# A two-block transformer on one core: first loads reordered, small tables issued behind x, and the adaLN modulation split 7 + 5 between two layers

## The chip, the cores and the metric

One Trainium2 chip; the program runs on one of its cores. The metric is device time in microseconds (us) of one execution. All arithmetic is float32. A float32 product is done as three TensorE passes: each operand is split into a high part `hi` (rounded to the type that TensorE reads in one pass) and a rest `lo = x - hi`, and `hi*hi + hi*lo + lo*hi` is accumulated.

## The reference, cut to what matters

There are 256 tokens of width 1024. A first block has two layers; a second block with state-space and sparse-attention mixers follows. A vector `c` of length 1024 modulates the second block:

```python
def first_block(x, mem, ...):
    x = layer_norm(x, emb_ln_g, emb_ln_b)
    for l in range(2):
        mixed = hybrid_mixer(x, mem, ...)      # conv, differential attention, attention over mem
        x = layer_norm(ALPHA * x + mixed, ln1_g[l], ln1_b[l])
        ff = square(relu(x @ w_up[l])) @ w_down[l]          # 1024 -> 4096 -> 1024
        x = layer_norm(ALPHA * x + ff, ln2_g[l], ln2_b[l])

def second_block(x, c, ...):
    mod = silu(c) @ ada_w + ada_b              # 1024 -> 6144, needs nothing of the first block
    shift_m, scale_m, gate_m, shift_f, scale_f, gate_f = split(mod, 6)
    h = rmsnorm(x, pre_norm_mix) * (1.0 + scale_m) + shift_m
    ...
```

`memory_attention` in both layers needs `mem @ w_mem_kv[l]` (256 x 1024 by 1024 x 512), which depends on no token.

## The kernel before, in words

**Weights.** Every weight arrives in units of 128 x 2048 floats (1 MB). `weight(...)` (line 242) loads a unit over SyncE's DMA queue into one of two `raw` buffers, in `parts` pieces, and then, in chunks of `cut` columns (1024 by default), ScalarE copies `raw` to `hi` (L255) and VectorE subtracts to `lo` (L256). There are four pairs of `hi`/`lo` buffers. So a load waits for a `raw` buffer that VectorE has finished with, and a split waits for a `hi`/`lo` pair that TensorE has finished with. The products are recorded on L261, L262 and L263, the transposes of tokens on L340.

**Order.** The program states operations and tiles. A planner in the compiler simulates the machine by its own cost figures and writes a fixed order of instructions for each engine and each DMA queue; the program's order is the priority among what the plan holds ready. At run time each engine and queue follows its fixed order, so an instruction whose operand is late holds up all behind it on its engine.

**Start.** `load()` brings `mem` (four pieces of 256 KB), the value weights of `mem` for layer 0 (two pieces of 512 KB), its key weights (1 MB), `x` (two of 512 KB) and the two rows of the first layer norm (512 KB each, as every partition gets a copy), all on SyncE's queue. `columns()` and `toeplitz()` bring small tables on GpSimd's queue: `cols` (256 KB), two copies of packed rows (32 and 256 KB), `shp` (224 KB), `hot` (64 KB) and `rb` (0.5 KB). None depends on anything, so they are issued in the first microseconds. GpSimd also does the power -0.5 of each layer norm (L309).

**Feed-forward of a layer.** Eight steps of 512 hidden channels. In step j the loop computes `up(j+1)` (two weight units, 96 matmuls of 256 columns) and the two `down` units of step j (48 matmuls of 512 columns), so that TensorE always has the next step's activations. After the loop come `up(7)` and the last four `down` units (12 to 15), with `close(t)` (residual, layer norm, transposes into `xT`) for each half of the tokens. PSUM holds four accumulators all the while.

**Modulation.** `silu(c) @ ada_w` is done on VectorE, not TensorE, in 12 parts of 512 columns. `modulation_part(n)` (L762) loads four pieces of 512 KB over SyncE's queue (L773) into two buffers tagged `s`, multiplies by a scalar of each partition and adds up (L777 once, L779 seven times), transposes 32 x 32 blocks (L781) and reduces (L782) into 16 columns of `modr`:

```python
        for h in range(4):
            w = self.new("s", [128, 2, 512])
            nc.sync.dma_start(out=w, in_=a["ada"][n, h])
            for k in range(2):
                ...   # acc (+)= w[:, k, :] * silu_c
        vec.transpose(out=t, in_=acc)
        vec.tensor_reduce(out=self.modr[:, 16 * n:16 * n + 16], ...)
```

Parts 0 to 5 lie in the six loop steps of layer 0, parts 6 to 11 in those of layer 1. `modulation_end()` sums the partitions with four small products on TensorE (L792, from `modr` and a table `place`), adds the bias (L795, L798), transposes (L800) and writes the gates out. Its result `modc` is first read in `modulated(0, ...)`, right after the first `close` of layer 1.

The functions that the diff touches, and what calls them:

## Time and profile before

| | before |
|---|---|
| median of 3 runs | 1275.21 us (1273.62 to 1282.3) |
| the profiled execution's own time | 1279.33 us |
| its span in the trace | 1277.6 us |
| TensorE matmul busy | 1203.1 us (94%) |
| VectorE busy | 966.1 us (76%) |
| ScalarE busy | 662.8 us (52%) |
| mean granted TensorE clock | 0.982 |
| moved by DMA | 247.81 MB, 194 GB/s on average |

The trace is one execution on the core. Times in it count from the span's start. "Busy" of TensorE is modelled from pipelined matmuls, so it is no measure of how near the engine is to its peak; gaps are read from the starts of instructions.

### The profile page before, as it was taken

How to read it: one execution, taken by the hardware profiler on the slowest of the kernel's cores; microseconds unless marked ns; L12 is line 12 of the kernel's file. 1: busy time of each engine (PE TensorE's matmuls, PEld its weight loads, DVE VectorE, ACT ScalarE, POOL GpSimd, SP SyncE). 2: the span in 40 equal slices, each digit the busy share in tenths (PEclk: the TensorE clock that was granted, in tenths of full speed). 3: DMA queues.
4: the chain of work that ended last, by engine and by line, in shares of the span. 5: the costliest groups of instructions: out<-in, count | busy, mean ns of one | idle time of the engine just before them, and what ended most of it. 6: DMA issues, size and time to landing. Idle time of an engine off the chain costs nothing.

```text
span 1277.6 us, 20408 instructions
## 1 busy us (share of the span) xinstructions
PE 1203.1 (94%) x8031; PEld 1064.6 (83%) x8031; DVE 966.1 (76%) x1741; ACT 662.8 (52%) x1082; POOL 65.2 (5%) x75
## 2 busy tenths in 40 slices
PE   6997989999999899999988899999999999999997
PEld 5886679899888568998877788789999968899996
DVE  5898577777789667787768995389999987655553
ACT  4546754444353875444335577555555634544441
POOL 2100000000000000000001000000111110000000
PEclk9998999999999899999989999999999999999999
DMA  8733567777561556777735344165454534554450
GB/s 310 263 138 122 191 217 261 253 294 278 198 239 67 190 189 242 273 272 256 279 105 192 120 161 167 70 243 190 164 185 185 185 110 159 198 199 180 183 198 33
DMA packets 53425, 247.81 MB, mean 194 GB/s; under 512 B 5277, under 2 KB 17597, under 8 KB 30545
## 3 DMA queue, kind: packets, MB, share of 16 engines
q1 hardware_dynamic: 52256, 243.22, 53.0%
q0 software_dynamic: 1072, 3.28, 0.8%
q8 instruction: 63, 1.03, 0.3%
q14 instruction: 34, 0.27, 0.1%
HBM read 241.06 MB, written 6.47 MB: 194 GB/s over the span
## 4 chain that ended last, share of the span: by engine, by line
PE 59%; DVE 18%; DMA 11%; ACT 7%; issue 4%; POOL 0%; SPq 0%; DVEq 0%; ACTq 0%; POOLq 0%
PE mm L263 11%; PE mm L262 11%; PE mm L261 11%; PE acc L263 7%; PE acc L261 7%; PE acc L262 6%; DVE lo L256 6%; DMA raw<-in_wts 6%; DVE cy L512 3%; DMA s<-in_ada 3%; ACT hi L255 3%; PE tr L340 1%; DVE t L779 1%; DMA rel<-reld 1%; DVE mask L1015 1%
## 5 line engine op out<-in xcount | busy, mean ns | idle before, releaser
L255 ACT ACTIVATE hi<-raw 128x1024 fp32r<-128x1024 f32 (+1 forms) x367 | 367.3, 1025 | 376.0 <-DMA raw<-in_wts 169.8
L256 DVE TENSOR_TENSOR lo<-raw,hi 128x1024 fp32r<-128x1024 f32 (+1 forms) x367 | 431.6, 1185 | 153.5 <-ACT hi L255 152.9
L261 PE MATMUL mm<-xT,hi 128*128 128x256 f32 x992 | 282.8, 285 | 2.6 <-DVE zs L1147 1.5
L263 PE MATMUL mm<-xT,lo 128*128 128x256 f32 x992 | 282.5, 285 | 0.0
L262 PE MATMUL mm<-xT,hi 128*128 128x256 f32 x992 | 282.1, 284 | 0.0
L261 PEld LDWEIGHTS mm<-xT,hi 128*128 128x128 f32 x992 | 191.8, 193 | 5.1 <-DVE zs L1147 1.7
L262 PEld LDWEIGHTS mm<-xT,hi 128*128 128x128 f32 x992 | 191.7, 193 | 0.8
L263 PEld LDWEIGHTS mm<-xT,lo 128*128 128x128 f32 x992 | 191.9, 193 | 0.2
L261 PE MATMUL acc<-hi,mh 128*128 128x512 f32 x320 | 127.8, 399 | 5.3 <-ACT mh L599 5.3
L262 PE MATMUL acc<-lo,mh 128*128 128x512 f32 x320 | 126.4, 395 | 0.0
L263 PE MATMUL acc<-hi,mh 128*128 128x512 f32 x320 | 125.9, 394 | 0.0
L262 PE MATMUL mm<-lo,xT 128*128 128x256 f32 (+1 forms) x288 | 85.7, 298 | 2.1 <-DVE lo L256 2.1
L263 PE MATMUL mm<-hi,xT 128*128 128x256 f32 (+1 forms) x288 | 86.4, 300 | 1.2 <-DVE xT L346 1.2
L261 PE MATMUL mm<-hi,xT 128*128 128x256 f32 (+1 forms) x288 | 87.1, 302 | 0.1
L779 DVE SCALAR_TENSOR_TENSOR t<-s,silu_c,t 128x512 f32<-128x512 f32 x84 | 62.9, 749 | 30.8 <-DMA s<-in_ada 30.3
L263 PE MATMUL mm<-h,lo 128*128 128x256 f32 x288 | 80.6, 280 | 0.0
L261 PE MATMUL mm<-h,hi 128*128 128x256 f32 x288 | 80.3, 279 | 0.0
L262 PE MATMUL mm<-h,hi 128*128 128x256 f32 x288 | 80.3, 279 | 0.0
L261 PEld LDWEIGHTS acc<-hi,mh 128*128 128x128 f32 x320 | 60.9, 190 | 18.7 <-ACT mh L599 6.1
L263 PEld LDWEIGHTS acc<-hi,mh 128*128 128x128 f32 x320 | 60.5, 189 | 13.8 <-issue 1.4
L262 PEld LDWEIGHTS acc<-lo,mh 128*128 128x128 f32 x320 | 60.7, 190 | 12.5 <-issue 1.1
L261 PEld LDWEIGHTS mm<-hi,xT 128*128 128x128 f32 x288 | 55.5, 193 | 5.2 <-issue 1.8
(382 smaller groups left out, 2220.7 us busy)
## 6 DMA issues: line engine op xcount, KB each, us to landing
raw<-in_wts SPq DMA_DIRECT2D x174, 1024.0 KB
s<-in_ada SPq DMA_DIRECT2D x48, 512.0 KB
rel<-reld SPq DMA_DIRECT2D x64, 64.0 KB
bias<-bo SPq DMA_DIRECT2D x16, 256.0 KB
bias<-bias SPq DMA_DIRECT2D x8, 512.0 KB
cr<-cumd SPq DMA_DIRECT2D x8, 512.0 KB
mh<-in_wts SPq DMA_DIRECT2D x3, 1024.0 KB
row<-in_ln_g SPq DMA_DIRECT2D x4, 512.0 KB
```

The costliest lines, as they stand in the source:

```text
L255: nc.scalar.activation(h[:, s], raw[:, s], AF.Copy)
L256: (lo_on or nc.vector).tensor_tensor(out=l[:, s], in0=raw[:, s], in1=h[:, s].bitcast(F32), op=OP.subtract)
L261: t.matmul(out=out, lhsT=l[0], rhs=r[0], start=start, stop=False)
L262: t.matmul(out=out, lhsT=l[0], rhs=r[1], start=False, stop=False)
L263: t.matmul(out=out, lhsT=l[1], rhs=r[0], start=False, stop=stop)
L340: self.nc.tensor.transpose(out=p[:, i, :], in_=x[:, i * 128:i * 128 + 128], identity=self.ident)
L512: vec.scalar_tensor_tensor(out=y, in0=u[:, c, j:j + 256], scalar=tap(j), in1=y, op0=OP.mult, op1=OP.add)
L779: vec.scalar_tensor_tensor(out=acc, in0=w[:, k, :], scalar=s, in1=acc, op0=OP.mult, op1=OP.add)
L1015: vec.scalar_tensor_tensor(out=isc, in0=rl[:, i, :], scalar=self.widx[:, t, h:h + 1], op0=OP.mult, op1=OP.add, in1=self.nadm[:, t, :] if h ...
```

## The change

1. `load()`: the value weights of `mem` for layer 0 come first, in four pieces of 256 KB with splits of 512 columns; `mem` goes to ScalarE's DMA queue.
2. `run()`: a one-column copy on GpSimd that reads `x[0]` is put ahead of `columns()` and `toeplitz()`, and every GpSimd instruction of these two is ordered behind it (`issue_after` adds order on that engine, no semaphore).
3. `layer()`: layer 0 takes modulation parts 0 to 6 (part 6 behind `up(7)`), layer 1 parts 7 to 11 in its first five steps; `modulation_end()` moves behind `up(7)` of layer 1.

```diff
     def load(self):
-        ms = []
+        wv = self.weight("mem", 0, 1, parts=4, cut=512)
         for t in range(NT):
             m = self.new("s", [128, D])
             for h in range(2):
-                nc.sync.dma_start(out=m[...], in_=a["mem"][...])
+                nc.scalar.dma_start(out=m[...], in_=a["mem"][...])
                 self.split_t(m[:, 512 * h:512 * h + 512], self.memT, 4 * h, t)
-            if t == 0:
-                wv = self.weight("mem", 0, 1, parts=2)
         wk = self.weight("mem", 0, 0)
...
+        self.gate = self.b1.tile([128, 1], F32, name="gate")
...
     def layer(self, l):
             hs.append(up(j + 1))
-            self.modulation_part(6 * l + j)
-            if 6 * l + j == 11:
-                self.modulation_end()
+            if 7 * l + j < 12:
+                self.modulation_part(7 * l + j)
             for i in range(2):
                 w = self.weight("down", l, 2 * j + i)
...
         hs.append(up(7))
         g, b = self.row(a["ln2_g"], D * l), self.row(a["ln2_b"], D * l)
         last = l + 1 == DEPTH
+        if last:
+            self.modulation_end()
+        else:
+            self.modulation_part(6)
...
     def run(self, stop=None):
             self.load()
-            self.columns()
-            self.toeplitz()
+
+            gate = nc.gpsimd.tensor_copy(self.gate, self.x[0][:, 0:1])
+            with tc.issue_after(gate.ins):
+                self.columns()
+                self.toeplitz()
```

## Rows read from the trace of the kernel before

**Rows 1.** The page's head and its first part: busy time of an engine, share of the span, instructions.

```profile
span 1277.6 us, 20408 instructions
PE 1203.1 (94%) x8031; PEld 1064.6 (83%) x8031; DVE 966.1 (76%) x1741; ACT 662.8 (52%) x1082; POOL 65.2 (5%) x75
```

**Rows 2.** Who waited for whom between 510 and 645 us, the feed-forward of layer 1: total us, how often, the longest.

```profile
PE tr L792 <- DVE modr L782: 7.3, 1, 7.3
```

**Rows 3.** TensorE's instructions in order of time near the end of layer 1's feed-forward: start us, us, engine, line, operation; in brackets the idle time before and what ended it.

```profile
635.48 0.28 PE L262 MATMUL mm<-xT,hi 128*128 128x256 f32 x1
643.03 1.94 PE L792 MATMUL tr<-modr,t 128*128 128x48 f32 x8 [7.27 <-DVE modr L782]
...
650.88 0.40 PE L261 MATMUL acc<-hi,mh 128*128 128x512 f32 x1
```

**Rows 4.** Busy time by stretches of 3 us there: stretch, length, then busy us (instructions) of PE, PEld, DVE, ACT and POOL, the granted TensorE clock, DMA share, GB/s.

```profile
636.00:639.00 3.00, 0.00 (x0) 0.00 (x0) 1.05 (x2) 1.03 (x2) 0.00 (x0) 0.96 0.72 274
639.00:642.00 3.00, 0.00 (x0) 0.00 (x0) 3.00 (x4) 1.30 (x2) 0.00 (x0) 0.50 0.10 41
...
645.00:648.00 3.00, 3.00 (x15) 2.96 (x16) 2.33 (x8) 0.63 (x1) 0.00 (x0) 0.50 0.25 104
```

**Rows 5.** VectorE's instructions in order of time, the ends of parts 10 and 11 and the wait in part 11.

```profile
616.57 0.69 DVE L782 TENSOR_REDUCE modr<-t 128x16 f32<-128x512 f32 x1
...
637.95 0.75 DVE L779 SCALAR_TENSOR_TENSOR t<-s,silu_c,t 128x512 f32<-128x512 f32 x1 [3.93 <-DMA s<-in_ada]
...
642.29 0.69 DVE L782 TENSOR_REDUCE modr<-t 128x16 f32<-128x512 f32 x1
```

**Rows 6.** TensorE in order of time, three first matmuls of `down` units: of step 0 in layer 0, of units 12 to 15 (behind the six steps) in layer 0, and of step 5 in layer 1.

```profile
200.82 0.40 PE L261 MATMUL acc<-hi,mh 128*128 128x512 f32 x1
...
335.34 0.40 PE L261 MATMUL acc<-hi,mh 128*128 128x512 f32 x1
...
617.26 0.40 PE L261 MATMUL acc<-hi,mh 128*128 128x512 f32 x1
```

**Rows 7.** The instructions of the modulation parts on VectorE, over the span: duration in ns (min/median/max), first and last start. The third is a group of 331 to 337 us: count, busy us, mean ns.

```profile
L779 DVE SCALAR_TENSOR_TENSOR t<-s,silu_c,t x84: 744/749/755, 203.8 to 639.8; 128x512 f32<-128x512 f32 x84
...
L777 DVE TENSOR_SCALAR t<-s,silu_c x12: 480/481/483, 199.7 to 620.6; 128x512 f32<-128x512 f32 x12
...
L781 DVE STREAM_TRANSPOSE t<-t 128x512 f32<-128x512 f32 x1 | 0.7, 707 | 0.0
...
L782 DVE TENSOR_REDUCE modr<-t x12: 685/686/689, 218.4 to 642.3; 128x16 f32<-128x512 f32 x12
```

**Rows 8.** Busy time by stretches at the end of layer 0's feed-forward (columns as in rows 4).

```profile
331.00:337.00 6.00, 6.00 (x46) 5.71 (x45) 4.97 (x6) 3.25 (x5) 0.00 (x0) 1.00 0.54 184
337.00:345.00 8.00, 8.00 (x37) 6.64 (x36) 4.39 (x6) 3.00 (x4) 0.00 (x0) 1.00 0.71 262
345.00:351.00 6.00, 6.00 (x28) 4.74 (x27) 5.71 (x13) 1.79 (x2) 0.92 (x1) 1.00 0.00 0
351.00:357.00 6.00, 5.99 (x30) 4.89 (x30) 6.00 (x7) 3.43 (x5) 0.00 (x0) 1.00 0.16 59
```

**Rows 9.** The same place in order of time, one row or two of SyncE's queue, VectorE, ScalarE and TensorE each: the last piece of part 5 issued, and waited for; a `down` unit issued, and waited for; TensorE at the second half's layer norm.

```profile
322.76 0.33 SPq L773 DMA_DIRECT2D s<-in_ada  x1
...
325.69 0.33 SPq L249 DMA_DIRECT2D raw<-in_wts  x1
...
328.24 0.75 DVE L779 SCALAR_TENSOR_TENSOR t<-s,silu_c,t 128x512 f32<-128x512 f32 x1 [1.91 <-DMA s<-in_ada]
...
333.18 1.06 ACT L255 ACTIVATE hi<-raw 128x1024 fp32r<-128x1024 f32 x1 [4.16 <-DMA raw<-in_wts]
...
365.08 1.29 PE L340 MATMUL tr<-ident,x 128*128 128x128 f32 x8 [0.79 <-DVE x L362]
```

**Rows 10.** Busy time by stretches at the start (columns as in rows 4).

```profile
0.00:4.00 4.00, 0.38 (x2) 0.41 (x3) 0.00 (x0) 1.28 (x1) 3.04 (x11) 1.00 0.42 141
4.00:8.00 4.00, 1.75 (x8) 1.02 (x6) 0.00 (x0) 0.00 (x0) 2.48 (x7) 1.00 0.95 261
8.00:12.00 4.00, 0.00 (x0) 0.00 (x0) 1.25 (x2) 2.17 (x3) 0.00 (x0) 1.00 1.02 356
12.00:16.00 4.00, 2.94 (x12) 2.65 (x13) 3.21 (x6) 1.03 (x3) 0.00 (x0) 1.00 0.99 386
...
20.00:24.00 4.00, 3.89 (x32) 3.89 (x33) 4.00 (x8) 0.80 (x3) 0.00 (x0) 1.00 1.03 426
...
28.00:32.00 4.00, 3.58 (x28) 3.16 (x27) 4.00 (x9) 3.68 (x6) 0.00 (x0) 1.00 0.41 138
```

**Rows 11.** The start in order of time, rows of GpSimd, ScalarE, VectorE and TensorE: a table issued, the first weights split, the first product, the `lambda` table used, the key weights of `mem`, the statistics of `x`, the first power -0.5.

```profile
3.52 0.56 POOL L399 DMA_DIRECT2D shp<-in_shp  x1
...
9.16 1.06 ACT L255 ACTIVATE hi<-raw 128x1024 fp32r<-128x1024 f32 x1 [7.14 <-DMA raw<-in_wts]
...
12.48 0.58 PE L261 MATMUL mm<-hi,mh 128*128 128x256 f32 x1 [6.73 <-ACT mh L345]
...
14.32 0.42 DVE L404 TENSOR_TENSOR t<-t 128x256 f32<-128x256 f32 x1
...
14.77 0.48 DVE L406 TENSOR_REDUCE sm<-t 128x2 f32<-128x128 f32 x2
...
17.14 1.06 ACT L255 ACTIVATE hi<-raw 128x1024 fp32r<-128x1024 f32 x1 [4.11 <-DMA raw<-in_wts]
...
21.71 1.87 DVE L329 BATCH_NORM_STATS2 sm<-x 128x6 f32<-128x512 f32 x3
...
24.45 0.94 POOL L309 TENSOR_TENSOR sm<-sm,mhalf 128x1 f32<-128x1 f32 x1 [17.97 <-DVE sm L333]
```

More of the change, by code (lines that the diff above doesn't have):

```diff
@@ L440, in load @@
             for h in range(2):
-                nc.sync.dma_start(out=m[:, 512 * h:512 * h + 512], in_=a["mem"][0, t * 128:t * 128 + 128, 512 * h:512 * h + 512])
+                nc.scalar.dma_start(out=m[:, 512 * h:512 * h + 512], in_=a["mem"][0, t * 128:t * 128 + 128, 512 * h:512 * h + 512])
                 self.split_t(m[:, 512 * h:512 * h + 512], self.memT, 4 * h, t)
-            if t == 0:
-                wv = self.weight("mem", 0, 1, parts=2)
         wk = self.weight("mem", 0, 0)
```

## The prediction, on record before the changed kernel ran

> **What bounds the kernel now.** I read the page first: TensorE is busy 94% of a span of 1277.6 us [rows 1], so the question is only where it is held up, and whether the change touches one of those places. It touches three: the first 30 us, the end of layer 0's feed-forward (335 to 370 us) and the end of layer 1's (617 to 675 us). For each I read the waits, then the order of instructions on the engine that waits, then busy time by short stretches.
>
> In the feed-forward loops TensorE is never short of weights. Layer 0 goes from the first `down` matmul of step 0 at 200.82 to that of units 12 to 15 at 335.34, six steps of 22.42 us [rows 6]. Modulation loads and VectorE work hide beside this until the end of layer 1. There TensorE stands still from 635.6 to 643.03 us in the middle of `up(7)`, because L792 is next in its order and waits for the last column sums of part 11 [rows 2, 3], which VectorE finishes at 642.98; part 11 in turn waited 3.93 us for a piece of `ada` [rows 5]. In the pause the granted clock falls from full to 0.50, the lower of TensorE's two levels (1.2 of 2.4 GHz), and it is still there from 645 to 648 us [rows 4]. This pause is the largest thing that the change can remove.
>
> **The change part by part.**
>
> *The end of layer 1.* After the change part 11 stands where part 10 stood, and part 10 ended at 617.26, 18 us before the pause [rows 5]; `modulation_end` is given a lower priority than all of `up(7)`. What is the pause worth? `down` of step 5 began at 617.26 [rows 6]. One step length later, at 617.26 + 22.42 = 639.68, the units 12 to 15 should begin, as they did in layer 0; they began at 650.88 [rows 3]. So 11.2 us are lost, of which the products of L792 and the transpose L800 would still take about 1.0 (the former 1.94 us at half clock, halved). Gain 10.2 us. The bounds: at least the bare pause of 7.3 less what may be left of it (rival 2), at most 11.2. Could the weights of units 12 to 15 be late instead? With no part in step 5, 2 MB less is in SyncE's queue and 7.1 us less on VectorE, and in layer 0 units 12 to 15 were fed on time with a part in step 5 [rows 6, 8]: I cost it at nothing. `modc` is wanted only after the first close, some 10 us behind. `place` comes on GpSimd, which has nothing else there. From here to the end every stage starts from TensorE's or VectorE's work before it, so I carry the 10.2 us through.
>
> *The end of layer 0.* Part 6 is new here. On VectorE it is 0.48 + 7 x 0.75 + 0.71 + 0.69 = 7.1 us [rows 7]. Four loads of 512 KB go into SyncE's queue between the loads of the `down` units. The cover: VectorE is idle 6 - 4.97 = 1.0 us from 331 to 337, 8 - 4.39 = 3.6 from 337 to 345 and 0.3 until 351, and none until 357 [rows 8], together 4.9. So 7.1 - 4.9 = 2.2 us must spill into the closes. There it is not hidden: the transposes of the second half already wait 0.79 us for VectorE [rows 9]. The loads: a piece of `ada` takes at most 328.24 - 322.76 = 5.5 us from issue to use, a `down` unit 333.18 - 325.69 = 7.5 [rows 9]. Two buffers hold the pieces, so the third is issued near 335 and used near 341, the fourth near 339 and 344 to 345. It just fits; if it misses, the last two pieces' four multiply-adds, the transpose and the reduction (4 x 0.75 + 1.4 = 4.4 us) lie wholly in the closes. Bounds 0 (the plan puts the rest into later gaps) and 5 (4.4, and the 0.79 us wait of TensorE for transposes once more); I take 2, the computed spill.
>
> Behind part 6 in SyncE's queue stand the loads of units 14 and 15 and the first weights of layer 1's mixer; a piece that waits for its buffer holds these up. In the loop steps the same order of four weights and four pieces is kept up at 22.42 us a step, so I take this as covered.
>
> *The start.* From 4 to 24 us the DMA engines are full: a share of 0.95 to 1.03 at 261 to 426 GB/s [rows 10]. The first weights are split at 9.16, the first product runs at 12.48, the key weights land at 17.14, and VectorE reaches the statistics of `x` at 21.71 [rows 11]; from 20 us on VectorE has no idle time [rows 10], so this start of its queue of work is what the next 30 us hang on. Deferring the tables takes 0.85 MB (256 + 32 + 256 + 224 + 64 KB) from ahead of `x`. What must land before VectorE can reach `x` is `mem`, both weight units of layer 0 and the positions, 3.28 MB. By the old rates 0.56 + 1.04 + 1.42 = 3.03 MB are moved at 12 us and 3.28 at 12.6 [rows 10], against 17.1 now. Then one `hi` (1.06) and two `lo` (1.2 each), so `x`'s statistics begin near 16.1: 5.6 us sooner. Against that, the two `lambda` steps that ran in VectorE's idle time (0.42 + 0.48, [rows 11]) now fall into its full time, and the smaller cuts add some 0.2. Gain 4.5 us. GpSimd must issue six tables at 0.56 us [rows 11], 3.4 us, just when the first power -0.5 comes due some 2.5 us after `x` lands; if the plan puts them ahead, the first layer norm waits up to 1 us. Bounds: -1 (a loss) and 6.
>
> That bytes come sooner only if others come later has a page behind it. The Trainium skill, "DMA: Bandwidth & Descriptors", section "Issuing engines are not separate DMA queues", says that DMAs started by SyncE, ScalarE and GpSimd run on the same 16 engines and interleave, so that a second issuing engine saves only issue time; its section "Queues, rings and completion order" says each DMA engine takes turns between the queues that have work. By that rule `mem` on ScalarE's queue takes half the rate from the "first" weights. No row here has loads of both queues at once, so the trace neither agrees nor disagrees. My sum counts both queues as one lump of bytes, which the rule allows; at its strictest (nothing but issue time saved) the term of the start is 0 and the sum -8.2, which is the first rival.
>
> *Elsewhere* the tables are first used at 45 us and later, which leaves 20 us of cover.
>
> **The sum.** -10.2 + 2 - 4.5 = -12.7 us. The profiled execution took 1279.33 (span 1277.6), 4.1 above the median of the runs, 1275.21; against the median the forecast is 1262.5, against the profiled execution 1266.6.
>
> **The rivals.**
>
> 1. *The start gains nothing.* The DMA engines are full beyond 24 us, the same bytes are wanted by 30 us, and the second pair of `mem` weights becomes what is late. For it: shares near 1.0 [rows 10]. Against it: 0.41 from 28 to 32 us, so the queue is not full for ever, and VectorE is busy for 1.25 of the first 12 us. Then -10.2 + 2 = -8.2: 1267.
>
> 2. *The change doesn't do what it says: the pause moves.* The plan put L792 too early once by 7.3 us; with `up(7)` ahead of it, it could still be put in front of a `place` load or a part 11 that runs late in step 4. For it: the plan's idea of time was wrong by that much. Against: part 11 has a whole step of slack. Half of the 10.2 remains: 1262.5 + 5 = 1267.5; all of it: 1272.7.
>
> 3. *Slower: part 6 starves TensorE in layer 0.* A piece of part 6 waits for its buffer at the head of SyncE's queue with units 14 and 15 behind it. TensorE then waits a full trip of a unit, 7.5 us [rows 9], for each of the two, the clock falls as it did at 639 us [rows 4] (3 us more: 6 us at half speed), and the closes start late by all of it: 18 us, against the 2 in my sum. Then -12.7 + 16 = +3.3: 1278.5. It decides when a piece's wait exceeds the lead of unit 14, which I estimate at 4 us: its `hi` begins at 333.18 [rows 9] and its split takes about 4 more (two `hi`, two `lo`, other work between); it is used 24 matmuls after 335.34, and with 48 of these and 96 of half their length in 22.42 us one takes 0.23, so at 340.9.
>
> **How the numbers follow.** Chances: forecast 0.55 (its own range 1257 to 1267: start 2 to 6, layer 0 cost 0 to 4), rival 1 0.2, rival 2 0.12, rival 3 0.06; 0.07 for a plan that differs in places I have not read, either way. The range of 8 in 10 runs from 1256 (all terms at their good ends) to 1271 (no gain at the start, layer 0 at 5 with half a pause left). 1% of 1275.21 is 12.75 us, about what a measurement of this kernel tells from no change; the forecast lies on that line, so faster by over 1% gets 0.48, within 1% 0.46, slower 0.06.
>
> **What would show it.** No wait of L792 on `modr`, and a granted clock of 1.00 through 630 to 650 us; units 12 to 15 of layer 1 one step length behind step 5's `down`. The statistics of `x` near 16 us. VectorE full from 337 to 357 us, and the first `down` of layer 0's units 12 to 15 still 134.5 us behind step 0. I'd be wrong if the end of layer 1 comes 10 us sooner relative to layer 0's end but the layers in between have grown, or if L792 still waits.

## The result, and the profile after

The changed kernel takes 1286.61 us (median of 11 runs, 1283.59 to 1288.6) where the kernel before, timed beside it, takes 1277.61: a ratio of 1.0069, 95% interval 1.005 to 1.0088. It is slower by 0.7%, 9 us, where the prediction had it 12.7 us faster; 1286.6 lies outside the range. The profiled execution took 1286.61 us, its span 1284.8 against 1277.6 [rows 1].

```profile
span 1284.8 us, 20415 instructions
PE 1207.1 (94%) x8031; PEld 1069.0 (83%) x8031; DVE 966.6 (75%) x1743; ACT 664.0 (52%) x1084; POOL 65.5 (5%) x76
```

VectorE and ScalarE are as busy as before and TensorE 4 us more, so 7.2 us of span must be found in waits and in the clock. I read them in order of time. In the changed kernel modulation_part's rows are L775 to L784 and modulation_end's products L794 (the edits move line numbers, so one operation has slightly different lines in different kernels).

**The start.** ScalarE, TensorE, VectorE and GpSimd of the changed kernel in order of time (start us, us, engine, line, operation; in brackets the wait and what ended it):

```profile
12.90 2.00 ACT L255 ACTIVATE hi<-raw 128x1024 fp32r<-128x1024 f32 x2 [1.99 <-DMA raw<-in_wts]
14.81 1.06 ACT L345 ACTIVATE mh<-tr 128x512 fp32r<-128x512 f32 x2
...
32.30 0.23 ACT L973 ACTIVATE brow<-brow 128x32 f32<-128x32 f32 x1 [2.94 <-DMA brow<-in_rows]
...
6.84 1.12 PE L340 MATMUL tr<-ident,s 128*128 128x128 f32 x4 [0.44 <-DMA s<-in_mem]
15.44 0.58 PE L261 MATMUL mm<-hi,mh 128*128 128x256 f32 x1 [7.48 <-ACT mh L345]
...
17.47 1.27 DVE L329 BATCH_NORM_STATS2 sm<-x 128x6 f32<-128x512 f32 x2
...
24.55 0.64 POOL L1372 COPY gate<-x 128x1 f32<-128x1 f32 x1 [1.97 <-DVE x L362]
25.13 0.60 POOL L389 DMA_DIRECT2D t<-in_cols  x1
```

The loads did what was forecast: key weights at 12.90 (17.14 before, 12.6 forecast), the statistics of `x` at 17.47 (21.71 before, 16.1 forecast; [rows 11]). But TensorE has transposed the first half of `mem` by 7.96 and waits until 15.44 for ScalarE to copy it, 3.0 us later than before: on ScalarE that copy (L345) stands behind the splits of the value weights *and* of the key weights. The products of `mem` pass this delay on: behind them the first product of layer 0's conv_in comes at 47.93, before at 45.23 (two rows, before and changed):

```profile
45.23 0.39 PE L261 MATMUL mm<-hi,xT 128*128 128x256 f32 x1
...
47.93 0.39 PE L261 MATMUL mm<-hi,xT 128*128 128x256 f32 x1
```

And the gate does not wait for the landing of `x[0]` but for its layer norm (L362), which overwrites the tile and stands earlier in the program. The tables go out at 25.1 and later, and ScalarE then stands 2.94 us in front of `brow`, with splits and copies behind it.

**The end of layer 0.** What TensorE waits for from 330 to 385 us (us in total, times, longest):

```profile
PE tr L340 <- DVE x L362: 5.1, 2, 2.8
PE acc L261 <- ACT mh L345: 1.3, 1, 1.3
```

VectorE there in order of time:

```profile
357.57 0.75 DVE L781 SCALAR_TENSOR_TENSOR t<-s,silu_c,t 128x512 f32<-128x512 f32 x1 [1.27 <-DMA s<-in_ada]
...
361.06 0.68 DVE L784 TENSOR_REDUCE modr<-t 128x16 f32<-128x512 f32 x1
361.65 0.21 DVE L312 SCALAR_TENSOR_TENSOR cl<-cl,cl 128x1 f32<-128x1 f32 x1
361.79 1.22 DVE L256 TENSOR_TENSOR lo<-raw,hi 128x1024 fp32r<-128x1024 f32 x1
362.92 0.15 DVE L316 SCALAR_TENSOR_TENSOR cl<-cl,cl 128x1 f32<-128x1 f32 x1
362.99 1.22 DVE L256 TENSOR_TENSOR lo<-raw,hi 128x1024 fp32r<-128x1024 f32 x1
364.12 1.41 DVE L362 SCALAR_TENSOR_TENSOR x<-x,cl,row 128x512 f32<-128x512 f32 x2
```

Part 6 does not spill out behind the closes, it stands inside the first one: its last piece waits 1.27 us at the head of VectorE's order in the middle of the layer norm, and two weight splits of 1.22 us have been planned in front of the last step, L362. TensorE waits 2.85 us for these rows and 2.22 for those of the second half, 5.1 in all (0.79 before, all of it for the second half, [rows 9]). Behind each of the two waits the granted clock falls to 0.50, which it does nowhere between 320 and 420 us in the kernel before (changed kernel, columns as in [rows 4]):

```profile
366.00:369.00 3.00, 3.00 (x10) 2.51 (x9) 2.56 (x4) 0.81 (x2) 0.00 (x0) 0.50 0.73 303
...
380.00:386.00 6.00, 5.42 (x26) 5.33 (x26) 3.04 (x5) 0.91 (x2) 0.00 (x0) 0.50 0.78 289
```

**The end of layer 1.** Busy time by 3 us in the changed kernel, columns as in [rows 4]:

```profile
636.00:639.00 3.00, 3.00 (x15) 2.49 (x14) 2.62 (x3) 2.42 (x4) 0.00 (x0) 1.00 0.77 317
639.00:642.00 3.00, 3.00 (x15) 2.49 (x14) 2.54 (x4) 2.50 (x3) 0.61 (x1) 1.00 0.45 137
```

Three rows of TensorE in order of time, the first `down` products of step 5 and of units 12 to 15 and the products of modulation_end:

```profile
634.34 0.40 PE L261 MATMUL acc<-hi,mh 128*128 128x512 f32 x1
...
656.76 0.40 PE L261 MATMUL acc<-hi,mh 128*128 128x512 f32 x1
660.65 1.01 PE L794 MATMUL tr<-modr,t 128*128 128x48 f32 x8
```

Here the forecast holds: no wait, clock 1.00, units 12 to 15 one step of 22.42 us behind step 5, where before it was 33.6 [rows 3, 6].

**A ledger.** The order of TensorE's instructions gives the same marks in every kernel: the first `down` product of layer 0, step 5's, the first product of layer 1's conv_in, the first `down` of layer 1, the first product of the second block. I read them for all kernels below (us between marks; the last column is the measured ratio with its 95% interval, each against runs of the kernel before on the same chip):

| kernel | layer 0's first down at | step 5's down to conv_in of layer 1 | mixer of layer 1 | first down of layer 1 to block 2 | ratio |
|---|---|---|---|---|---|
| before | 200.8 | 45.5 | 146.8 | 169.6 | 1 |
| after | 204.7 | 52.7 | 152.7 | 159.4 | 1.0069 (1.005, 1.0088) |
| e1 feed-forward part alone | 197.5 | 52.2 | 150.8 | 159.7 | 1.0000 (0.9976, 1.0024) |
| e2 both edits of the start | 202.7 | 46.3 | 149.0 | 172.2 | 1.0057 (1.0035, 1.008) |
| e4 gate on the landing | 203.9 | 46.4 | 149.4 | 169.5 | 1.0048 (1.0026, 1.0069) |
| e6 weights first alone | 201.0 | 48.9 | 149.5 | 168.1 | 1.0047 (1.0019, 1.0074) |
| e8 gate alone | 195.3 | 49.7 | 148.2 | 169.7 | 1.0031 (1.0006, 1.0055) |
| e9 as e6, copies first | 206.4 | 51.5 | 147.9 | 170.1 | 1.0071 (1.0044, 1.0097) |
| e10 as e9, with the gate | 200.0 | 47.4 | 149.4 | 172.1 | 1.0056 (1.0037, 1.0075) |
| e5 as e1, part 6 loaded by GpSimd | 195.2 | 54.2 | 150.0 | 160.8 | 0.9997 (0.9972, 1.0021) |
| e12 as e1, part 6 loads only | 200.4 | 51.3 | 148.4 | 164.6 | 0.9956 (0.9934, 0.9979) |
| e13 as e1, part 6 work only | 202.1 | 57.2 | 148.7 | 159.4 | 0.9963 (0.9939, 0.9986) |
| e11 as e1, part 6 in the mixer | 200.0 | 49.9 | 160.9 | 160.9 | 1.0005 (0.9981, 1.0028) |
| e3 modulation_end moved | 196.5 | 46.7 | 147.1 | 168.3 | 0.9970 (0.995, 0.999) |
| e7 and `place` early | 198.9 | 48.5 | 146.8 | 166.3 | 1.0006 (0.9976, 1.0037) |
| e14 part 11 left out | 197.4 | 49.6 | 146.7 | 166.2 | 0.9945 (0.9921, 0.9969) |
| e15 modulation_end behind 48 downs | 200.4 | 49.6 | 151.3 | 162.3 | 0.9976 (0.9951, 1.0000) |

The table is also a warning. The ten kernels with the old start have the same plan up to here, but for one or two small instructions, and reach layer 0's first `down` anywhere from 195.2 to 202.1 us (mean 198.9). Most of this is TensorE's waits (24.3 to 31.1 us in all) and stretches at the lower clock (6.8 to 10.2 us lost, an estimate: the time, times what the mean granted clock lacks to 1). Both taken off, 160.4 to 163.6 us are left. One profile stands for one execution; below some 4 us a difference between two profiles says little, and only the ratio or a mean over several kernels does.

### The profile page after: what moved, and what is told of

It reads as the page before. It is cut to its first block, busy times and chain, and to the rows that moved or that the text cites. A ratio compares the mean times of both kernels' runs of the same rounds, so it can differ in the third digit from the quotient of the medians.

```text
span 1284.8 us, 20415 instructions
## 1 busy us (share of the span) xinstructions
PE 1207.1 (94%) x8031; PEld 1069.0 (83%) x8031; DVE 966.6 (75%) x1743; ACT 664.0 (52%) x1084; POOL 65.5 (5%) x76
## 4 chain that ended last, share of the span: by engine, by line
PE 59%; DVE 17%; DMA 12%; ACT 6%; issue 5%; POOL 1%; SPq 0%; DVEq 0%; ACTq 0%; POOLq 0%
PE mm L261 11%; PE mm L263 11%; PE mm L262 11%; DMA raw<-in_wts 6%; PE acc L263 6%; PE acc L262 6%; PE acc L261 6%; DVE lo L256 6%; DMA s<-in_ada 3%; ACT hi L255 3%; DVE cy L511 2%; PE tr L340 1%; DVE t L781 1%; DMA rel<-reld 1%; DVE mask L1017 1%
## 5 line engine op out<-in xcount | busy, mean ns | idle before, releaser
L255 ACT ACTIVATE hi<-raw 128x1024 fp32r<-128x1024 f32 (+2 forms) x369 | 367.6, 1020 | 370.7 <-DMA raw<-in_wts 169.6
L256 DVE TENSOR_TENSOR lo<-raw,hi 128x1024 fp32r<-128x1024 f32 (+2 forms) x369 | 431.1, 1177 | 150.0 <-ACT hi L255 149.4
L261 PE MATMUL mm<-hi,xT 128*128 128x256 f32 (+1 forms) x288 | 89.4, 310 | 0.4 <-ACT xT L345 0.3
L263 PE MATMUL mm<-hi,xT 128*128 128x256 f32 (+1 forms) x288 | 88.4, 307 | 1.3 <-DVE xT L346 1.3
L262 PEld LDWEIGHTS acc<-lo,mh 128*128 128x128 f32 x320 | 61.2, 191 | 12.7 <-issue 1.1
```

The costliest lines, as they stand in the source:

```text
L255: nc.scalar.activation(h[:, s], raw[:, s], AF.Copy)
L256: (lo_on or nc.vector).tensor_tensor(out=l[:, s], in0=raw[:, s], in1=h[:, s].bitcast(F32), op=OP.subtract)
L261: t.matmul(out=out, lhsT=l[0], rhs=r[0], start=start, stop=False)
L262: t.matmul(out=out, lhsT=l[0], rhs=r[1], start=False, stop=False)
L263: t.matmul(out=out, lhsT=l[1], rhs=r[0], start=False, stop=stop)
```

## Experiments: the two halves of the change

**e1** is the part of the diff in the feed-forward alone, **e2** the two edits of `load()` and `run()` alone.

> The kernel before with the feed-forward part of the change alone (seven modulation parts in layer 0, five in layer 1, modulation_end after up(7)); its start is untouched. Theory A, read from the two traces: the end of layer 0 costs 10.75 us and layer 1's end gives 10.2 back, and layer 1's mixer loses 2.4 us more: in sum 0.5 to 3 us above the kernel before, 1278 to 1281 us where that takes 1277.6. In its trace the first matmul of conv_in of layer 1 comes 9 to 12 us later than before, counted from the first down matmul of layer 0. Theory P, the prediction: 2 us lost at the end of layer 0 and 10.2 gained, 8.2 us faster, 1269.4 us.

> The kernel before with the two edits of the start alone (first weights ahead of everything and the mem tiles on ScalarE's queue; the small tables behind the gate on x). Theory A, read from the two traces: layer 0's feed-forward begins 3.9 us later, and nothing gives that back: 3.9 us slower, 1281.5 us where the kernel before takes 1277.6. Theory P, the prediction: 4.5 us faster, 1273.1. Rival 1 of the prediction: no change within 1 us.

Measured: e1 1.0000, e2 1.0057, 7.3 us (4.5 to 10.3) of 1282.55. So the loss is the start's, and the feed-forward part comes out even within 3 us: in e1's ledger layer 0's end and the mixer lose what layer 1's end gains. The prediction's terms for both halves fall. Theory A has the sign of e2, but its 3.9 us, from one pair of profiles, was too little. For e1 its 0.5 to 3 us lie within the interval, while its sign in the trace was missed: conv_in of layer 1 comes 6.8 us later, counted from layer 0's first `down`, not 9 to 12.

## Experiments: the start

**e4**, against e2: the gate's copy is written between the loads of `x` and the layer norm.

```
         self.gate = self.b1.tile([128, 1], F32, name="gate")
+        self.gated = nc.gpsimd.tensor_copy(self.gate, self.x[0][:, 0:1])
...
-            gate = nc.gpsimd.tensor_copy(self.gate, self.x[0][:, 0:1])
-            with tc.issue_after(gate.ins):
+            with tc.issue_after(self.gated.ins):
```

**e6** is the first hunk of the diff alone (first weights ahead, `mem` on ScalarE's queue), **e8** the gate alone.

> The two edits of the start alone, with the gate's copy written in the program between the loads of x and the layer norm, so that it waits for the landing of x[0] and not for its normalised rows; the tables then go out near 17 us and not at 25.1. Theory A1: the late tables are the cause of what the start loses (ScalarE's wait of 2.9 us for brow with the splits behind it, the conv weights behind the rel loads): most of the 3.9 us goes, the time is within 1.5 us of the kernel before or below it, and ScalarE shows no wait for brow. Theory A2: the loss comes from the order of mem's copies behind the weight splits on ScalarE (first product at 15.4 us in place of 12.5): it stays at 3 to 4 us whatever the gate waits for.

> The kernel before with the first edit of the start alone: the first weights ahead of everything, mem on ScalarE's queue, no gate, tables issued at once. Theory A2 (ScalarE's order): the copies of the transposed mem stand on ScalarE behind all splits of the value weights and those of the key weights, so the first product comes at 15.0 to 15.6 us in place of 12.48 whatever the tables do: 3 to 7 us slower than the kernel before, most of what both edits together lost (7.3 us by their ratio 1.0057). Theory A1 (late tables): the first edit alone costs nothing, within 1.5 us of the kernel before, and the loss is the gate's. The prediction: some 4 us faster.

> The kernel before with the second edit of the start alone: the small tables behind the gate, first weights and mem as before. Theory A2: first product at 12.5 us as before, less load beside the first weights; within 2 us of the kernel before. Theory A1: ScalarE waits 2 to 3 us for brow near 30 us with splits behind it, and toep and the rel loads come late: 3 to 7 us slower.

Measured: 1.0048, 1.0047 and 1.0031. In e4 GpSimd copies at 14.83, the tables go out from 15.8, and ScalarE waits 4.24 us for `brow` all the same, at 23.62; the time is within error of e2's. So the late opening of the gate is not the main cause. In e6, without any gate, TensorE's first wait is longer than in the changed kernel. What TensorE waits for until 30 us in e6:

```profile
PE mm L261 <- ACT mh L345: 10.4, 1, 10.4
```

And ScalarE in order of time in e6:

```profile
15.65 2.00 ACT L255 ACTIVATE hi<-raw 128x1024 fp32r<-128x1024 f32 x2 [3.27 <-DMA raw<-in_wts]
17.56 1.06 ACT L345 ACTIVATE mh<-tr 128x512 fp32r<-128x512 f32 x2
```

The copy of `mem` stands behind key weights that land at 15.65 here, as the tables' loads run beside them (12.90 with the gate). The first product comes at 18.19, beyond A2's 15.0 to 15.6: I had left out that without the gate the loads are slower. The gate alone (e8) keeps the first product at 12.28 and brings `x`'s rows 2.5 us sooner, and its profile is the earliest of all but one at 195.3; yet 12 timed runs put it 4.0 us (0.8 to 7.0) above the kernel before. The time lies in A1's range of 3 to 7 us, but ScalarE's wait for `brow` is 0.66 us there and not 2 to 3. That contradiction between one profile and the times stays open.

**e9** and **e10** put the key weights' splits behind the copies of `mem`'s first half, on ScalarE alone, without and with the gate (`copied` is the last L345 of that half):

```
-        wk = self.weight("mem", 0, 0)
+        with self.tc.issue_after(copied.ins):
+            wk = self.weight("mem", 0, 0)
```

> The first edit of the start (weights first, mem on ScalarE's queue, no gate) with one order more on ScalarE: the splits of the key weights stand behind the copies of mem's first half. Loads and their queues stay as in the run of the first edit alone. Theory A2: the copies follow the last split of the value weights (10.3 us + 0.6) in place of the key weights' (13.0 + 2.0), so the first product comes at 11.3 to 12.2 us, and what the first edit lost is gone: within 1.5 us of the kernel before, or up to 3 us faster since x lands earlier. If the loss is not from that order (contention of the loads, the table load of ScalarE behind its DMA issues), the time stays where the first edit alone has it.

> Both edits of the start, and the splits of the key weights behind the copies of mem's first half on ScalarE, as in the run of that order without the gate. There the first product came at 14.3 us and not at 11.3 to 12.2, since the tables' loads ran beside the value weights, whose last two quarters were split at 10.25 and 13.15; with the gate the quarters come at 8.6 and 10.3. Theory A2 (ScalarE's order, once the loads come early): first product at 11.4 to 12.2 us, and the 7.3 us that both edits lose fall to 0 to 3 us, ratio 1.000 to 1.0025. Rival L (the order of loads as a whole: mem, value and key weights share the engines and land together, so that the products run out of operands a few us later): the first product comes early and a gap opens behind it, the ratio stays at 1.004 to 1.008.

Measured: 1.0071 and 1.0056; what the order on ScalarE should have given back did not come. In e9 the first product is at 14.31 and not at 11.3 to 12.2, as the last quarter of the value weights is split at 13.15 only. In e10 the first product is at 11.91, as forecast, but then (e10 in order of time, TensorE and VectorE):

```profile
11.91 0.58 PE L261 MATMUL mm<-hi,mh 128*128 128x256 f32 x1 [4.01 <-ACT mh L345]
...
16.10 1.12 PE L340 MATMUL tr<-ident,s 128*128 128x128 f32 x4 [3.39 <-DVE mh L346]
...
14.76 0.69 DVE L329 BATCH_NORM_STATS2 sm<-x 128x6 f32<-128x512 f32 x1 [2.66 <-DMA x<-in_x]
15.37 1.27 DVE L346 TENSOR_TENSOR mh<-tr,mh 128x512 fp32r<-128x512 f32 x2
```

VectorE's order has the statistics of `x` ahead of the `lo` half of `mem` (L346), so it waits 2.66 us for `x` to land while `mem` lies ready, and TensorE with it. The wait moved from one engine's order to the next. In the kernel before L346 runs at 13.12 and `x` comes after. A2 falls. Rival L's signs came true, an early first product, a gap behind it and a ratio within its range; but the rows show the gap where VectorE's order has a load that is still under way ahead of work that is ready. No run mends the order on both engines, so that the order on two engines is the cause is argued, not shown.

What the start costs by the traces: 203.8 us on average at layer 0's first `down` with both edits (after, e2, e4) against 198.9 with the old start, 4.8 us. The times say 7.3 (4.5 to 10.3); whether the rest is real stays open. TensorE's order from conv_in on is the same in e6, e2 and the changed kernel as before, but the order of SyncE's queue is not. The second weight unit of conv_in (`mh`) went out ahead of the position tables (`rel`), first two rows, before; in the changed kernel it stands behind the first of them, last two rows:

```profile
43.83 0.33 SPq L249 DMA_DIRECT2D mh<-in_wts  x1
46.31 2.33 SPq L875 DMA_DIRECT2D rel<-reld  x4
...
47.42 1.79 SPq L877 DMA_DIRECT2D rel<-reld  x3
49.31 0.41 SPq L249 DMA_DIRECT2D mh<-in_wts  x1
```

SyncE waits 6.2 us for `reld` before that `rel`, and the unit goes out 5.5 us later than before. TensorE then waits 3.2 us ahead of the transposes behind this unit's products (2.0 before), and the clock falls (changed kernel; 1.00 in the kernel before):

```profile
PE tr L340 <- DVE t L485: 3.2, 1, 3.2
...
59.00:65.00 6.00, 5.34 (x25) 5.35 (x26) 2.52 (x4) 2.88 (x4) 0.79 (x1) 0.50 0.49 169
```

The same order and a clock of 0.50 near 60 us are in e2, e4, e6 and e10, and in none of the ten with the old start nor in e8. No run changes this order alone, so what it costs is not shown.

## Experiments: what part 6 costs at the end of layer 0

**e5**: part 6's loads on GpSimd's queue. **e12**: its loads without its arithmetic. **e13**: its arithmetic without its loads.

e5, e12 and e13 against e1:

```
-            nc.sync.dma_start(out=w, in_=a["ada"][n, h])
+            (nc.gpsimd if n == 6 else nc.sync).dma_start(out=w, in_=a["ada"][n, h])
```
```
+        if n == 6:
+            for h in range(4):
+                w = self.new("s", [128, 2, 512])
+                nc.sync.dma_start(out=w, in_=a["ada"][n, h])
+                vec.tensor_copy(self.modr[:, 16 * n + 4 * h:16 * n + 4 * h + 4], w[:, 0, 0:4])
+            return
```
```
+            if n == 6:
+                w = self.toep.rearrange("p a b -> p (a b)")[:, 0:1024].rearrange("p (k c) -> p k c", k=2)
+            else:
                 w = self.new("s", [128, 2, 512])
                 nc.sync.dma_start(out=w, in_=a["ada"][n, h])
```

> The feed-forward part of the change alone, as in the run of that part, with one difference: the four loads of modulation part 6 are issued on GpSimd's queue and not on SyncE's. The arithmetic of part 6 on VectorE stays where it is. Theory Q (queue): most of the 10 us lost at the end of layer 0 come from weight loads that stand in SyncE's queue behind pieces of ada waiting for a buffer; then the shift from entering layer 0's feed-forward to conv_in of layer 1 falls from 10 to 2 to 4 us, and the kernel becomes 5 to 8 us faster than before, ratio 0.994 to 0.996. Theory V (VectorE): the loss comes from the 7.1 us of part 6's work among the closes; the shift stays at 8 to 11 us and the ratio at 1.00, as with the loads on SyncE's queue.

> The feed-forward part of the change alone, with part 6 cut to its loads: its four pieces of ada are loaded at the end of layer 0, but in place of their eight multiply-adds, the transpose and the reduction VectorE copies four columns of each piece (so this part of the modulation is left out). Measure: the time from the first down product of step 5 of layer 0 to conv_in's first product of layer 1, 52.2 to 54.2 us in the runs with part 6 there and 45.5 to 49.9 us without. Theory B (bytes): the last up weights come late because ada's 2 MB share the DMA engines; TensorE still waits 3 us or more before units 12 to 15, and the stretch stays at 50.5 to 53 us. Theory V (VectorE's work and the order around it): no wait above 1 us is left in the closes and the stretch falls to 46 to 49 us.

> The feed-forward part of the change alone, with part 6 cut to its work: all its operations on VectorE stay, but they read a table that is in the chip already (toep), and its four loads are gone (so this part of the modulation is computed from other numbers). Theory B: TensorE's wait before units 12 to 15 is gone and the stretch from step 5's first down product to layer 1's conv_in falls to 46 to 49.5 us. Theory V: it stays at 51 to 54 us, with waits for x's normalised rows in both closes. Both at once: each of the two runs loses part of it, 48.5 to 51 us in both.

What TensorE waits for from 325 to 385 us, in e1:

```profile
PE tr L340 <- DVE x L362: 4.0, 2, 2.5
PE acc L261 <- ACT mh L345: 2.2, 1, 2.2
```

The same in e5, with the loads on the other queue:

```profile
PE tr L340 <- DVE x L362: 3.9, 2, 2.2
PE acc L261 <- ACT mh L345: 3.6, 1, 3.6
```

In e12, with the loads alone:

```profile
PE acc L261 <- ACT mh L345: 2.8, 1, 2.8
PE tr L340 <- DVE x L362: 0.8, 1, 0.8
```

In e13, with the work alone:

```profile
PE tr L340 <- DVE x L362: 4.2, 2, 2.7
PE acc L261 <- ACT mh L345: 2.7, 2, 2.5
```

Theory Q falls: with another queue nothing changes, neither the waits nor the ratio (0.9997). The wait for `x`'s rows in the closes is VectorE's: 3.9 to 5.1 us whenever part 6's arithmetic is there, 0.8 as before when it isn't. It needs no late piece of `ada`: in e13 the operands lie in the chip, yet VectorE's order puts six of the eight multiply-adds behind the work for the activations of `up(7)`, just ahead of the first close:

```profile
352.44 4.69 DVE L785 SCALAR_TENSOR_TENSOR t<-toep,silu_c,t 128x512 f32<-128x512 f32 x6
```

The other wait, for the activations of `up(7)` (L345) at units 12 to 15, is not part 6's alone: it is 2.7 us without part 6's loads (e13), 2.3 in e9, which has no part 6 there at all, and absent in e2 and in the kernel before. It hangs on when the last `up` weights land, and that scatters from one execution to the next; theory B's sign, 3 us or more of this wait, tells nothing. The ledger's second column is 45.5 to 51.5 us in the twelve kernels without part 6 there (mean 48.3) and 53.0 on average in the three with all of it, 4.7 us more. The column ends between the two closes, so the second half's wait is in the next one. Three things make up its differences: the wait for the activations, the wait for the first half's rows (1.5 to 2.9 us with part 6's arithmetic, none otherwise) and the clock. Taking off all waits and what the lower clock loses (the estimate above), 45.1 to 46.8 us are left in each of the 17 kernels. So theory V's and theory B's ranges for this column decide nothing: e12 has 51.3 by 2.8 us of waits and 3.4 of clock, e13 has 57.2, the longest of all, by 7.0 and 3.4.

By the times both halves count: e12 is 5.6 us and e13 4.7 us faster than the kernel before, e1 is not; taking out either gives back about half of the 10 us. Where the loads' half sits no row shows: the wait for the activations is 2.8 us in e12 and 2.7 in e13.

**e11** puts part 6 into layer 1's mixer, behind the loop over heads; against e1:

```
+        if l == 1:
+            self.modulation_part(6)
         bo = self.row(a["b_out"], D * l)
```

> The feed-forward part of the change alone, with part 6 placed in layer 1's mixer, behind the last head pair's values and ahead of the weights of the output product, and not at the end of layer 0; parts 7 to 11 in steps 0 to 4 of layer 1 and modulation_end behind up(7), as in the change. In the trace of before VectorE is busy 2.89, 0.00 and 2.79 of 6 us from 438 to 456 us, and the DMA engines' share is 0.56, 0.19 and 0.50. Theory: 18 us of which VectorE stands idle 12 take the 7.1 us of part 6, the end of layer 0 is as before, and the 10.2 us of the end of layer 1 are kept: 7 to 10 us faster than before, ratio 0.992 to 0.9945. Rival: the pieces of ada wait at the head of SyncE's queue for the buffers that the scores hold, with the output weights behind them, or part 6 stands ahead of the softmax's work on VectorE: 3 to 10 us are lost in the mixer, ratio 0.997 to 1.001.

Measured: 1.0005, the rival's side. The mixer grows to 160.9 us from 148.4, the mean of the eleven kernels that have part 6 neither there nor at layer 0's end. From 430 to 510 us TensorE waits

```profile
PE tr L340 <- DVE x L362: 3.8, 1, 3.8
PE acc L261 <- ACT mh L599: 2.9, 1, 2.9
PE tr L883 <- ACT step L880: 2.6, 3, 2.1
```

where in the kernel before the first was 0.6, the second the same and the third not among the long ones. These waits are 6.5 us more over the mixer than in the kernel before; the granted clock is 0.92 on average there and was 0.98, by the same estimate up to 10 us more. VectorE's idle time there was real, but SyncE's queue carries the position tables (`rel`) for the next products, and in e11's plan the pieces of `ada` stand among them. That this is what makes the rows late was not tested.

## Experiments: what the pause at the end of layer 1 is

**e3** moves modulation_end behind `up(7)` and leaves six parts in each layer; **e7** adds a buffer of its own for `place`; **e14** leaves out part 11; **e15** moves modulation_end behind the `down` products of the first half.

All four against the kernel before. e3, and e15, which both take modulation_end out of the loop:

```
         last = l + 1 == DEPTH
+        if last:
+            self.modulation_end()
```
```
             self.downs(acc[t], [(hs[6 + i // 2], (2 * (i % 2), 2 * (i % 2) + 1)) for i in range(4)], ws, t, False)
+            if last and t == 0:
+                self.modulation_end()
```

e7 (on e3) and e14:

```
+            self.place = self.b1.tile([128, 4, 128], F32, name="place")
+            nc.gpsimd.dma_start(out=self.place, in_=a["place"])
```
```
-            self.modulation_part(6 * l + j)
+            if 6 * l + j < 11:
+                self.modulation_part(6 * l + j)
```

> The kernel before with one step of the change: modulation_end stands after up(7), and six modulation parts stay in each layer, part 11 in step 5 of layer 1. Theory A: the pause of TensorE came from the place of L792 in its order alone, since part 11's sums are there at 642.98 us, and up(7) with nothing in its middle ends near 643: the pause goes and 10 us are gained, without the price that part 6 has at the end of layer 0: 1267.5 us where the kernel before takes 1277.6. Rival: with part 11 in step 5 its pieces stand in SyncE's queue ahead of units 12 to 15, or L792 still waits for it in its new place, and the pause only moves: a gain of 0 to 5 us, 1272.6 to 1277.6, with a wait of TensorE of 3 us or more between 635 and 655 us.

> The kernel before with modulation_end behind up(7), as in the run of that step alone, and the table place in a buffer of its own, loaded with the first modulation part and not when a buffer of the ring t2 comes free (641.9 us, landing near 646). Theory: in that run the pause had moved behind up(7) and was 5.33 us long, waiting for place alone; with place there early only part 11's sums are left to wait for (941 ns or so after up(7)'s last product): a pause of at most 1.5 us, and 7 to 10 us faster than the kernel before, ratio 0.992 to 0.9945, where the step alone gave 0.997. Rival: the pause moves again, to the weights of units 12 to 15 (hi and lo of them waited 1.4 us at 646.8), and the gain stays at 3 to 4 us, ratio 0.997.

> The kernel before with modulation part 11 left out altogether (its 16 columns are set to zero), modulation_end where it was. Nothing pays for it elsewhere. The prediction's first term: the pause before L792 goes, the stretch from step 5's first down product in layer 1 to the second block's first product falls from 57.5 us to 47 to 49 us as in the change, and the whole time by 9 to 11 us, ratio 0.9915 to 0.993. Rival: the stretch falls, but the measured time by less than half of it (ratio 0.996 to 1.000), because later stages give it back.

> The kernel before with one step: modulation_end stands behind the down products of the first half (units 12 to 15), six modulation parts stay in each layer. L792 then has 48 products of 128x512, 11 us by the loop's 11.07 us for as many, between the end of up(7) near 641 us and itself, and part 11's sums (642 to 645 us) and place (landing near 646) are both there. Theory: no wait at L792, full clock, and the time from layer 1's first down product to the second block's first product falls from 169.6 us to 159.4 to 161 us, as in the kernels with seven and five parts; nothing is paid elsewhere, so the measured time falls by 8 to 11 us, ratio 0.9915 to 0.994. Rival: the last up weights are late by themselves (their pieces of ada are ahead of them), TensorE waits before units 12 to 15 in place of L792, and only 3 to 5 us are gained, ratio 0.996 to 0.9975.

What TensorE waits for at modulation_end's products (L792 to L794 by kernel) from 610 to 675 us, in e3:

```profile
PE tr L792 <- DMA t<-in_place: 5.3, 1, 5.3
```

In e7:

```profile
PE tr L793 <- DVE modr L784: 3.8, 1, 3.8
```

In e14:

```profile
PE tr L794 <- DMA t<-in_place: 2.4, 1, 2.4
```

The pause has several layers. Move the products alone and they wait for `place`, whose load needs a `t2` buffer that part 11 holds until 641.9. Give `place` its own buffer and they wait for part 11's sums. Leave part 11 out and the plan puts the products earlier, where `place` is late again. All three gain 1.3 to 3.4 us in that stretch of the ledger against the one profile of the kernel before; the seven kernels with the old end have 168.1 to 172.2, so e3's 168.3 is within their scatter. Their times differ by more than these traces explain (0.9970, 1.0006, 0.9945). e3 comes out as its rival had it. e7 gains nothing, less than both its theory and its rival. e14's ratio lies between its two forecasts, and its theory's 47 to 49 us for the stretch from step 5 on became 54.1. Only two things take the wait at these products away: a step more for part 11, as in the change (159.4 to 160.9 in five kernels; 164.6 in e12, which has no wait at them but 3.5 us at the transpose behind them), or 48 products in front of modulation_end, as in e15, which has no wait at L792 and a clock of 1.00 in this stretch (e15 by 6 us, columns as in [rows 4]):

```profile
642.00:648.00 6.00, 6.00 (x52) 6.00 (x52) 2.17 (x4) 2.00 (x2) 0.00 (x0) 1.00 0.76 289
648.00:654.00 6.00, 5.94 (x27) 4.55 (x26) 5.96 (x9) 3.13 (x4) 0.61 (x1) 1.00 0.50 179
654.00:660.00 6.00, 4.29 (x17) 2.62 (x16) 4.19 (x6) 3.12 (x4) 0.00 (x0) 1.00 0.72 225
```

Its stretch is 162.3, 7 us below before; 1.7 us are left as waits from 654 to 660 us, for weights of `up(7)` that land behind part 11's pieces, as its rival had it. By time e15 gains 3.1 us (0 to 6.3) and e3 3.8 (1.3 to 6.4): both beat the changed kernel, and e3 the kernel before as well (e15's interval reaches no gain), with no part moved. e15's theory, 8 to 11 us, is missed; its rival's 3 to 5 holds.

## Why the prediction was wrong, step by step

- **End of layer 1, a gain of 10.2: right.** After's stretch is 159.4 against 169.6, and the mean over the six kernels that have part 11 a step earlier is 9.4 below that of the seven with the old end (160.8, 170.2). That the one pair agrees to the tenth is luck: the scatter within either group is 4 to 5 us. For the change as it was the mechanism, part 11 a step ahead and L792 behind `up(7)`, is what the rows show. L792's place in the order alone gave 1.3 us (e3), where `place`, put at nothing as GpSimd is free, waits for a buffer until 641.89; what worked was part 11's extra step.
- **End of layer 0, a cost of 2 with bounds 0 to 5: mis-sized.** 4.7 us in that stretch, near the upper bound, and some 3 more behind conv_in's first product, in the mixer's column (151.2 with part 6 at layer 0's end, 148.4 without, scatter 146.7 to 151.3). The step that failed is "4.9 us of idle cover": idle time of VectorE was subtracted from part 6's 7.1 us as if the arithmetic could flow into it. It couldn't: in the changed kernel the last piece comes at 357.57, when the gaps are over, and the plan puts the rest of part 6, with two splits, into the chain from the accumulators to `x`'s rows, which TensorE waits for; e13 shows the same wait where no piece is late. The sum also had no term for the clock, which falls behind both closes and loses some 5 us between 365 and 386 us in the changed kernel (10 us at 0.50). Rival 3 had such a term.
- **The start, a gain of 4.5: wrong in sign, and the main error.** It lost 7.3 us (e2). The two terms that were worked out came nearly true (12.90 for 12.6, 17.47 for 16.1), but the sum followed `x` only. The step that failed is "this start of its queue of work is what the next 30 us hang on": TensorE's first product was named at 12.48 and never carried through the change. It hangs on ScalarE's copy of `mem`, and in the new order that copy stands behind the key weights' splits: 15.44. This delay is still there at conv_in's first product (47.93 against 45.23), although `x`'s rows come sooner (L362 at 23.77 against 26.69). It is not the whole loss: with the first product at 11.91 (e10) conv_in's is at 47.17 all the same and the time stays, and what holds the rest is argued (VectorE's order, SyncE's order at 47 us), not shown. The lower bound of -1 looked only at GpSimd.
- **"Elsewhere the tables are first used at 45 us": wrong.** The prediction's own [rows 11] have VectorE use a table at 14.32, and ScalarE takes the `brow` table at 12.80 in the kernel before, a row that I did not follow; in the changed kernel it stands 2.94 us there. The gate was also taken to open when `x` lands; it opens when `x` is normalised, at 24.55, where in e4, which waits for the landing, it opens at 14.83.
- **The page on queues** (the Trainium skill, "DMA: Bandwidth & Descriptors", "Issuing engines are not separate DMA queues"). Now rows bear on it, and they agree: in e6, which has the first hunk alone, the last quarter of the "first" value weights is split at 11.75, where the last half was split at 10.89 before. Being first, with `mem` on another queue, bought nothing there; 10.28 in the changed kernel has the tables held back as well.
- **Rivals.** Of the start, rival 1 (it gains nothing) was nearest and still too kind. Rival 2's mechanism, products waiting for `place` or for part 11, is what e3 and e7 show, but not the change. Rival 3's time (1278.5) was the nearest, and its clock falls came; but it named a queue, e5 shows that it wasn't the queue, and its price of 18 us was too high. No rival had the start slower than before.

## What to carry to other kernels

When loads are brought forward in a kernel with a fixed order on each engine, follow the first product back through each engine's order, not only the load you moved: what was early and ready (here `mem`) is held by what the plan has put in front of it (here the key weights on ScalarE, then `x` on VectorE). Idle time of an engine is cover only for work that the engine's fixed order puts into it; having the operands early was not enough (e13). Work put between an accumulator and the rows that the next stage reads held TensorE up for 3 to 4 us of its 7.1, and the lower clock behind the waits there cost the changed kernel about as much again: count both. Before moving the work that makes a product late, try moving the product: 48 other products in front of it took the wait away.

## What the runs showed that I had not expected

- Executions scatter where TensorE waits, and not at all where it doesn't: a loop step lasts 22.42 us in layer 0 in all 17 kernels, while the first 200 us, of nearly the same instructions, lasted 195.2 to 202.1 us, and the second block, which no kernel here touches, 594.6 to 600.0.
- Small tables weigh on large loads: with them beside the first weights the key weights were split at 15.65 us, with them held back at 13.02, all else alike (e6 and e2).
- A 7 us change of the start shows in the times (e2) but less in the traces (4.8 us as a mean of three against ten), and the gate alone shows in the times only. I have no cause for that.
